# A smaller descriptor area for GpSimd's DMAs, and with it a lower start of every tile on the left side of SBUF

## The chip, the cores and the metric

The kernel runs on one core of a Trainium2 chip. The metric is the device time of one execution in microseconds (us). Each engine works through its own list of instructions in order: TensorE (PE) multiplies, VectorE (DVE), ScalarE (ACT) and GpSimd (POOL) do the elementwise work, and SyncE (SP) issues most of the DMAs. They meet at semaphores. SBUF is the memory from which the engines work; an address in it is given below as a byte offset within one partition.

## What is computed

One layer of a streaming encoder on 2048 rows of 1024 numbers, in float32. A mixer with two groups of heads (differential attention, and a gated linear recurrence called HGRN2) is followed by an output projection with a residual, and that by a convolutional gated feed-forward with a second residual. Cut to its frame:

```python
h = _rmsnorm(x, ln1_w[l])
proj = h @ w_in[l]
...
o_diff = _diff_attention(dq, dk, dv, lam, lam_init, diff_subln_w[l])
...
o_hgrn = _hgrn2(..., hg, lb, hgrn_norm_w[l])
x = x + jnp.concatenate([o_diff, o_hgrn], axis=-1) @ w_out[l]
x = x + _conv_ffn(_rmsnorm(x, ln2_w[l]), w_up[l], conv_w[l], conv_b[l], w_down[l])
```

In the attention a row sees all chunks of 64 rows up to its own, so the last block of rows has the most to do.

## The kernel before

The program has four stages, each with its own set of tile pools.

1. **The mixer** (lines 200 to 546). Four passes `s` over the heads; in each pass eight blocks `b` of 256 rows. `proj_a`, `proj_b` and `proj_c` are the input projections (L269 to L271), `attn` makes the scores `sc` of a block of 128 rows in segments of up to 1024 columns (L379, L380), takes their negated maximum `nm` on DVE (L387) and the exponential `p` on ACT (L398). There is one `sc` buffer (`SCB` is 1), so the scores of the next segment wait until the exponential has read this one. `attn_o` mixes the two softmaxes (L425, DVE), transposes the result (L431, PE), copies it (L433, ACT) and multiplies it with the values (L436, PE); the norm of the result goes over ACT (L440), POOL (L103, L105) and DVE (L443, L444), and L445 stores 128 columns of it in `o_d[i]`. `hgrn` and `hgrn_o` (L447 to L510) do the recurrence and store into the same `o_d[i]` by L510.
2. **The output projection** (lines 549 to 634). For each block `i` of 128 rows `load_o` loads `o_d[i]` into `ot` (L564) and the rows of x into `xt` (L566), transposes `ot` (L572) and splits it into a high and a low part `oT` (L577, L578). 48 matmuls (L621 to L623, two halves of 24) multiply it with `w_out`, L624 adds the residual on DVE, L625 stores the sum, and L628, L103, L105 and L630 make its norm `ht`. `tail` transposes `ht` (L590) and scales it into `hs` (L593). The eight row groups of `w_out` are split by `prep_wo` (L196 on ACT, L197 on DVE or POOL), seven of them late in the mixer, into tiles that held the projection weights, and the eighth (`wo7`, line 558) into a tile of its own.
3. **The up projection and the convolution** (lines 641 to 744), and 4. **the down projection** (lines 747 to 889). In stage 4 L838 adds partial results to `x2_d` in HBM by DMAs that POOL issues with `accum_op`; these 48 are the only DMAs of the program that POOL issues.

The order in which the instructions of each engine stand isn't that of the Python code: the build moves instructions of a later stage forward between those of an earlier one, as far as tiles and operands allow. A pool is laid at the left end of SBUF (from low addresses up) or at the right end (from high addresses down, `side="right"`). Pools of a later stage take addresses that pools of an earlier stage held; with `reuse_waits="tile"` (L84) a tile that takes over bytes waits for the last use of the tiles that had them.

```python
wk = pool(ms, "wk", 2, side="right")          # L206, mixer
sm = pool(ms, "sm", 4, side="right")          # L207, mixer: its small tiles
hp = pool(ms, "hp", 2, side="right")          # L210, mixer: hT
wp = pool(ms, "wp2", 1)                       # L551, output projection: wo7
wk = pool(ms, "wk2", 1)                       # L552: ot, xt, oT, ht
sm = pool(ms, "sm2", 4)                       # L553: ss2, r2_m, r2_r
```

At address 0 lies the area in which the descriptors of POOL's DMAs are written; the left pools begin behind it. `bacc.Bacc` takes its size per partition as `dynamic_dma_scratch_size`, 16384 where nothing is said.

## Time and profile before

| | us |
|---|---|
| three timed runs | 2781.37, 2786.12, 2788.0 (median 2786.12) |
| the profiled execution | 2784.47 |
| span of the profiled execution | 2782.5 |
| PE busy | 2651.1 (95%) |
| DVE, ACT, POOL busy | 1900.4 (68%), 1262.0 (45%), 1053.8 (38%) |

The page divides the span into 40 slices of 69.6 us and gives the busy tenths of each engine and the TensorE clock that was granted, in tenths of full speed. Matmul ends are modelled and overlap the next start, so for PE the distance between two starts tells what one costs.

### The profile page before, as it was taken

To read this page: it belongs to the slowest core of one execution; us is meant where nothing else is said; L and a number is where in the kernel's file an instruction comes from. 1 tells how busy PE (TensorE), PEld (TensorE's weight loads), DVE (VectorE), ACT (ScalarE), POOL (GpSimd) and SP (SyncE) were. 2 spreads that over 40 slices of the span, in tenths; PEclk is the share of its full clock that TensorE was granted. 3 is DMA by queue.
4 is the path that set the end of the run, shared out by engine and by line. 5 is a ranking of instruction groups with operands and counts; after the bars stand their busy time and mean duration, and the time that the engine had idled before them with its cause. 6 is when DMAs were issued, how large, how long until landed. Compare 5 with 4: busy or idle time off the path is not lost. (4 is left out here: it accounts for less than half of the span.)

```text
span 2782.5 us, 42697 instructions
## 1 busy us (share of the span) xinstructions
PE 2651.1 (95%) x14722; PEld 2303.3 (83%) x14722; DVE 1900.4 (68%) x4058; ACT 1262.0 (45%) x3095; POOL 1053.8 (38%) x1168
## 2 busy tenths in 40 slices
PE   7999999999999999969999999999999998899999
PEld 6888899989999999858877888887888886687887
DVE  5667856676568666752337666669677678977787
ACT  5556544564456445532334443435344344434332
POOL 3221222222222222310325344343443446887775
PEclk9999999999999999979999999999999999999999
DMA  5323422242223232114765222225222224775754
GB/s 190 121 97 111 132 85 88 80 133 84 84 84 112 85 114 83 51 37 152 237 204 159 82 78 91 79 81 176 90 91 72 88 89 120 166 165 132 174 173 171
DMA packets 273492, 322.92 MB, mean 116 GB/s; under 512 B 19470, under 2 KB 238974, under 8 KB 269182
## 3 DMA queue, kind: packets, MB, share of 16 engines
q1 hardware_dynamic: 266366, 295.04, 32.4%
q0 software_dynamic: 6912, 25.17, 5.3%
q8 instruction: 117, 1.92, 0.3%
q14 instruction: 97, 0.79, 0.1%
HBM read 198.50 MB, written 104.86 MB: 109 GB/s over the span
## 5 line engine op out<-in xcount | busy, mean ns | idle before, releaser
L706 PE MATMUL q<-xT,WS 128*128 128x512 f32 x704 | 274.1, 389 | 1.6 <-DVE xT L639 1.6
L707 PE MATMUL q<-xT,WS 128*128 128x512 f32 x704 | 274.2, 389 | 0.6 <-DVE WS L639 0.6
L705 PE MATMUL q<-xT,WS 128*128 128x512 f32 x704 | 274.0, 389 | 0.7 <-ACT WS L638 0.7
L819 PE MATMUL pd<-TW,SG 128*128 128x512 f32 x616 | 244.7, 398 | 19.6 <-DVE acc L825 6.7
L821 PE MATMUL pd<-TW,SG 128*128 128x512 f32 x616 | 243.0, 395 | 3.3 <-DVE SG L639 3.3
L820 PE MATMUL pd<-TW,SG 128*128 128x512 f32 x616 | 243.7, 396 | 0.9 <-DVE TW L639 0.7
L638 ACT CAST WS<-st 128x512 fp32r<-128x512 f32 x176 | 108.4, 618 | 240.9 <-PE q L707 229.7
L706 PE MATMUL q<-xB,WS 128*128 128x512 f32 x528 | 206.5, 391 | 2.6 <-DVE xB L639 2.5
L705 PE MATMUL q<-xB,WS 128*128 128x512 f32 x528 | 206.6, 391 | 2.3 <-ACT xB L638 2.3
L707 PE MATMUL q<-xB,WS 128*128 128x512 f32 x528 | 205.9, 390 | 0.0
L398 ACT ACTIVATE p<-sc,nm 128x1024 f32<-128x1024 f32 (+4 forms) x192 | 165.4, 862 | 76.8 <-DVE nm L387 75.7
L639 POOL TENSOR_TENSOR WS<-st,WS 128x512 fp32r<-128x512 f32 x44 | 87.5, 1989 | 278.9 <-ACT WS L638 278.9
L387 DVE TENSOR_REDUCE nm<-sc 128x1 f32<-128x1024 f32 (+4 forms) x192 | 173.9, 906 | 12.6 <-PE sc L380 10.7
L269 PE MATMUL pj<-WA,hT 128*128 128x384 f32 x512 | 176.6, 345 | 2.6 <-DVE hT L256 2.6
L270 PE MATMUL pj<-WA,hT 128*128 128x384 f32 x512 | 174.6, 341 | 0.0
L271 PE MATMUL pj<-WA,hT 128*128 128x384 f32 x512 | 174.5, 341 | 0.0
L436 PE MATMUL av<-vst,aT 128*128 128x128 f32 x1088 | 152.7, 282 | 8.2 <-ACT aT L433 7.8
L819 PEld LDWEIGHTS pd<-TW,SG 128*128 128x128 f32 x616 | 117.7, 191 | 49.8 <-DVE acc L825 8.1
L706 PEld LDWEIGHTS q<-xT,WS 128*128 128x128 f32 x704 | 132.1, 188 | 29.7 <-DVE xT L639 2.5
L707 PEld LDWEIGHTS q<-xT,WS 128*128 128x128 f32 x704 | 132.1, 188 | 28.8 <-DVE WS L639 1.5
L705 PEld LDWEIGHTS q<-xT,WS 128*128 128x128 f32 x704 | 132.1, 188 | 28.6 <-ACT WS L638 1.2
L638 ACT CAST WS<-rawu 128x512 fp32r<-128x512 f32 x132 | 81.9, 622 | 161.1 <-PE q L707 159.9
(441 smaller groups left out, 7896.3 us busy)
## 6 DMA issues: line engine op xcount, KB each, us to landing
hT<-hTd SPq DMA_DIRECT2D x24, 2048.0 KB, 7.9
rawu<-in_w_up_dram SPq DMA_DIRECT2D x176, 256.0 KB, 3.1
x2d<-acc POOLq DMA_DIRECT2D x48, 512.0 KB, 6.5
gd<-c SPq DMA_DIRECT2D x176, 128.0 KB, 1.8
G<-gd SPq DMA_DIRECT2D x24, 768.0 KB, 4.3
hTd<-hT SPq DMA_DIRECT2D x8, 2048.0 KB, 6.2
qT<-qh SPq DMA_DIRECT2D x256, 64.0 KB, 2.0
rawd<-in_w_down_dram SPq DMA_DIRECT2D x22, 512.0 KB, 4.4
```

Source lines behind the costliest of these rows:

```text
L269: PE.matmul(dst, lhsT=lh, rhs=rh, start=dt == 0, stop=False)
L270: PE.matmul(dst, lhsT=lh, rhs=rl, start=False, stop=False)
L271: PE.matmul(dst, lhsT=ll, rhs=rh, start=False, stop=dt == ND - 1)
L387: DVE.tensor_reduce(out=nm, in_=sc[:, 0:w], axis=AX.X, op=ALU.max, negate=True)
L398: ACT.activation(out=p[:, 0:w], in_=sc[:, 0:w], func=AF.Exp, bias=nm, accum_out=l)
L638: ACT.copy(dst[:, 0], src)
L705: PE.matmul(dst, lhsT=w[:, 0, cs], rhs=b_[:, 0, dt], start=dt == 0, stop=False)
L706: PE.matmul(dst, lhsT=w[:, 0, cs], rhs=b_[:, 1, dt], start=False, stop=False)
L707: PE.matmul(dst, lhsT=w[:, 1, cs], rhs=b_[:, 0, dt], start=False, stop=dt == 3)
L819: PE.matmul(pd, lhsT=Sx[n][:, 0, k], rhs=w[:, 0], start=k == 0, stop=False)
L820: PE.matmul(pd, lhsT=Sx[n][:, 0, k], rhs=w[:, 1], start=False, stop=False)
L821: PE.matmul(pd, lhsT=Sx[n][:, 1, k], rhs=w[:, 0], start=False, stop=k == len(qs) - 1)
```

## The change

The descriptor area takes 8192 bytes per partition. Nothing else in the text of the kernel is touched.

```diff
-    nc = bacc.Bacc("TRN2", target_bir_lowering=False, num_devices=1)
+    nc = bacc.Bacc("TRN2", target_bir_lowering=False, num_devices=1, dynamic_dma_scratch_size=8192)
```

All left pools of all stages start 8192 bytes lower; the right pools stay. As the build lays the tiles out, in bytes of a partition:

| pool | side, stage | before | with the change |
|---|---|---|---|
| `hp` (`hT`) | right, mixer | 94208 to 126976 | the same |
| `sm` (small tiles) | right, mixer | 133440 to 136164 | the same |
| `wp2` (`wo7`) | left, output projection | 93184 to 101376 | 84992 to 93184 |
| `wk2`: `ot`, `xt`, `oT` | left, output projection | 101376 to 130048 | 93184 to 121856 |
| `wk2`: `ht` | left, output projection | 130048 to 134144 | 121856 to 125952 |
| `sm2` | left, output projection | 134336 to 134628 | 126144 to 126436 |

So `ht` and `sm2` no longer share bytes with the mixer's `sm`, and `wo7` no longer with `hT`. `ot`, `xt` and `oT` share bytes with `hT` before and after. All offsets move by a multiple of 512 bytes, the unit to which `Rows` (L41 to L59) rounds its tiles.

The order of the instructions changes in one place of the program, the end of the mixer's last pass and the start of the output projection. On all engines it is the same before and behind it. Three pieces:

PE, in the scores of the last rows of the mixer (`sc`, L379 and L380; `lt`, L465, is the recurrence; `pjo` is the output projection, here of block 0):

```order
 L379 MATMUL sc<-kst,qT 128x384
 L380 MATMUL sc<-kst,qT 128x384
+L621 MATMUL pjo<-woWA,oT 128x512
+L622 MATMUL pjo<-woWA,oT 128x512
+L623 MATMUL pjo<-woWA,oT 128x512
+L621 MATMUL pjo<-woWA,oT 128x512
+L465 MATMUL lt<-qP,kp 128x128
+L622 MATMUL pjo<-woWA,oT 128x512
+L623 MATMUL pjo<-woWA,oT 128x512
```

All 48 matmuls of block 0 now stand among the last score groups: 15 between this group and the next, then 13, 10, 9, and the last one behind the scores. Before, none of them stood ahead of the mixer's last matmul.

PE, the end of the mixer (`av`, L436, is its last product; `tpo` are the transposes of `load_o`, `tph` those of `tail`):

```order
 L431 MATMUL tpa<-ident,p 128x128 x8
+L590 MATMUL tph<-ident,ht 128x128 x2
 L436 MATMUL av<-vst,aT 128x128 x8
-L572 MATMUL tpo<-ident,ot 128x128 x8
+L590 MATMUL tph<-ident,ht 128x128 x6
 L621 MATMUL pjo<-woWA,oT 128x512
 L622 MATMUL pjo<-woWA,oT 128x512
```

Behind the mixer's last product there now come six transposes of block 0's `tail` and then the matmuls of block 1, whose own transposes (L572) stand ahead of it.

SP, the stores of the mixer's last rows (`od` numbered by block of 128 rows, `rawu` a load for stage 3) and the loads of the output projection (`ot` from `od_97` and `xt` for block 0, `od_98` for block 1):

```order
+L668 DMA rawu<-in_w_up_dram 128x4x128 x2
+L445 DMA od_109<-oo 128x128
+L564 DMA ot<-od_97 128x1024
+L566 DMA xt<-in_x_dram 128x1024 x2
 L668 DMA rawu<-in_w_up_dram 128x4x128
-L445 DMA od_109<-oo 128x128
-L668 DMA rawu<-in_w_up_dram 128x4x128 x2
 L510 DMA od_109<-o_16488 128x128
+L564 DMA ot<-od_98 128x1024
 L445 DMA od_110<-oo 128x128
 L510 DMA od_110<-o_16511 128x128
+L510 DMA od_111<-o_16834 128x128
```

Before, the loads L564 and L566 all came behind the store of `od_112`, the mixer's last; now three of them stand right behind the store of `od_109`, and that of `ot` for block 1 two rows on. On ACT and DVE the cast and the difference of `wo7` (L196, L197) move ahead by some ten instructions, and the splits, sums and the norm of block 0 (L577, L578, L624, L628, L630) now stand among the last instructions of `attn`.

## Rows read from the trace of the kernel before

**Rows 1.** From the page's 40 slices: PE, and the granted clock of TensorE.
```profile
PE   7999999999999999969999999999999998899999
...
PEclk9999999999999999979999999999999999999999
```

**Rows 2.** Windows: start and end, length, busy us (count) per engine, PEclk, DMA share, GB/s.
```profile
1200.00:1210.00 10.00, 5.94 (x16) 4.40 (x16) 6.46 (x23) 2.77 (x7) 0.74 (x2) 0.59 0.04 13
1210.00:1220.00 10.00, 6.80 (x19) 5.19 (x20) 8.29 (x27) 2.48 (x5) 0.00 (x0) 0.50 0.01 2
1220.00:1230.00 10.00, 8.90 (x59) 7.94 (x58) 4.84 (x16) 5.60 (x15) 0.74 (x2) 0.89 0.00 0
1230.00:1240.00 10.00, 5.79 (x27) 4.92 (x28) 5.69 (x13) 3.18 (x9) 3.39 (x4) 0.62 0.07 20
1240.00:1250.00 10.00, 5.35 (x34) 4.92 (x33) 0.51 (x2) 1.53 (x4) 0.74 (x2) 0.84 0.11 29
```

**Rows 3.** Waits of PE from 1188.5 to 1254.5: total us, times, longest.
```profile
PE tpo L572 <- DMA ot<-od: 6.3, 1, 6.3
...
PE sc L379 <- ACT p L398: 3.5, 2, 3.3
```

**Rows 4.** Timeline of PE: start, us, instruction, idle before it and its releaser.
```profile
1243.53 2.05 PE L436 MATMUL av<-vst,aT 128*128 128x128 f32 x16 [0.24 <-ACT aT L433]
1251.90 1.97 PE L572 MATMUL tpo<-ident,ot 128*128 128x128 f32 x8 [6.32 <-DMA ot<-od]
1254.42 0.79 PE L621 MATMUL pjo<-woWA,oT 128*128 128x512 f32 x1 [0.55 <-DVE oT L578]
...
1262.51 0.39 PE L621 MATMUL pjo<-woWA,oT 128*128 128x512 f32 x1
...
1267.95 0.60 PE L572 MATMUL tpo<-ident,ot 128*128 128x128 f32 x4
...
1269.31 0.47 PE L621 MATMUL pjo<-woWA,oT 128*128 128x512 f32 x1
...
1275.09 1.03 PE L590 MATMUL tph<-ident,ht 128*128 128x128 f32 x8
1275.88 0.48 PE L622 MATMUL pjo<-woWA,oT 128*128 128x512 f32 x1
```

**Rows 5.** Timeline of SP: DMA issues.
```profile
1191.28 0.92 SPq L668 DMA_DIRECT2D rawu<-in_w_up_dram  x2
...
1247.65 0.32 SPq L445 DMA_DIRECT2D od<-oo  x1
1248.02 0.42 SPq L564 DMA_DIRECT2D ot<-od  x1
```

**Rows 6.** Timeline of PE: the last score matmul of a segment and the next segment's first.
```profile
1213.72 0.63 PE L380 MATMUL sc<-kst,qT 128*128 128x512 f32 x1
...
1217.15 0.80 PE L379 MATMUL sc<-kst,qT 128*128 128x512 f32 x1
```

**Rows 7.** Timelines of DVE and PE: single instructions whose lengths are used.
```profile
1196.29 1.22 DVE L197 TENSOR_TENSOR wo<-raw,wo 128x1024 fp32r<-128x1024 f32 x1
...
1233.88 2.47 DVE L425 SCALAR_TENSOR_TENSOR p<-p,cc 128x1024 f32<-128x1024 f32 x2
...
1253.67 0.69 DVE L578 TENSOR_TENSOR oT<-tpo,oT 128x512 fp32r<-128x512 f32 x1 [6.05 <-ACT oT L577]
...
1236.49 1.94 PE L431 MATMUL tpa<-ident,p 128*128 128x128 f32 x8 [1.71 <-DVE p L425]
1238.26 3.78 PE L436 MATMUL av<-vst,aT 128*128 128x128 f32 x16
```

**Rows 8.** The page's queue of POOL's DMAs, and the issues of L838.
```profile
q0 software_dynamic: 6912, 25.17, 5.3%
...
L838 POOL DMA_DIRECT2D x2d<-acc x48: 861/1128/1197, 2352.9 to 2676.3; - x48
...
DMA to landing us min/median/max: 5.2/6.5/11.2
```

## The prediction, on record before the changed kernel ran

> **What bounds the kernel now.** I read the page first. PE is busy nine tenths or more in nearly every slice, at full clock nearly everywhere; the one dent in both lies in the 18th slice, 1183 to 1252 us [rows 1]. Where PE is dense, a change pays only if it takes work or idle time off PE. So the next view is the windows of PE there: from 1200 to 1250 it is busy 5.4 to 8.9 us of each ten, and the granted clock is 0.50 to 0.89 of full [rows 2]. This is the place that the change touches: the mixer's last rows, where its other work has run out.
>
> The waits say what holds PE there: one hole of 6.3 us for the load of `ot`, and waits for a chain through DVE and ACT, the longest 3.3 for an exponential [rows 3]. The timelines put them in order. The mixer's last product ends at 1243.53 + 2.05 = 1245.58; PE then stands until 1251.90 and transposes block 0 [rows 4]. The load was issued at 1248.02, on SP right behind the store of the mixer's last rows at 1247.65 [rows 5]: the output projection begins only when the mixer is over. Its first 24 matmuls take from 1254.42 to 1262.51, 8.09 us, the next 24 until 1267.95, 5.44 or 0.227 each [rows 4]. The second is the full clock of 2.4 GHz; the first was paid partly at 1.2 GHz, the level of the window 1210 to 1220 [rows 2].
>
> **The change, term by term**, from the profiled execution (2784.47 us; the median of the timed runs lies 1.65 higher).
>
> *What leaves the path: 24.5 us.* Block 1's matmuls begin at 1269.31. In the new order they follow the mixer's last product with only six transposes (L590) between, and the eight L590 of block 0, which stood inside block 1's matmuls for 1275.88 - 1275.09 = 0.79 [rows 4], have moved ahead too. So 1269.31 + 0.79 - 1245.58 = 24.52 us lie between the two points: the wait for the mixer's last norm and store, the load, the transposes and block 0's 48 matmuls.
>
> *What comes back there: 0.8 us,* the eight L590; 1.6 at half clock.
>
> *The clock at block 1's start: 0.5 us.* Block 0 lost 8.09 - 5.44 = 2.65 to the low clock. Block 1 follows the mixer's products without a hole, and of these the last 16 took 2.05 [rows 4] where the 16 before them took 3.78 [rows 7]: PE was back at full some 2 us ahead of its end. I take 0.5 and keep 0 and 2.6 as ends.
>
> *The mixer's tail itself: 1 us earlier.* Here 48 matmuls and 16 transposes (L572) are put among the scores. From the last score matmul of one segment to the first of the next (DVE's maximum and ACT's exponential lie between) PE has 1217.15 - 1213.72 - 0.63 = 2.8 us free [rows 6]. The groups of 15, 13, 10 and 9 moved matmuls need 3.4, 3.0, 2.3 and 2.0 us at 0.227; with 0.3 for `lt` the first two overflow, by 0.9 and 0.5. Against that, filled holes should give the full clock: four score matmuls then take 4 x 0.227 = 0.9 us less per segment, and four segments ran at half (0.59 and 0.50 from 1200 to 1220 [rows 2]): 3.6 back. On DVE two splits (L578) and two sums (L624), 0.69 each [rows 7], come among the maxima; DVE is idle a third of 1200 to 1230 [rows 2], and I count one of them on the chain, 0.7. In front, the difference of `wo7` (1.22 [rows 7]) now stands ahead of the mixing of an earlier block; it no longer stands where it stood, so 0.5 net. 3.6 - 1.4 - 0.7 - 0.5 = 1.0; the bounds are 3 earlier and 2 later.
>
> *SP.* The load of `ot` moves past the stores of three blocks of rows. Ahead of it stands the pair of `rawu`, which waited for DVE until 1191.28 [rows 5] and now waits some 1 us more for the later difference. Issued near 1193.3 and landing about 3.9 us later (1251.90 - 1248.02 [rows 4, 5]), it lets the first transpose go at about 1197. That one stands in PE's list between a score group's two halves and what precedes them; PE stands some 2 us, but DVE's next maximum waited for the norm of earlier rows as well, so I leave it within the bounds above. The stores that now follow the load wait for later data in any case. Block 1's load waits for block 0's transposes near 1200 and has 30 us of cover. POOL takes two small norm steps ahead of the last recurrence's, whose store nothing of the path waits for; the cast of `wo7` on ACT moves ahead by some 10 us, and its data were issued well before.
>
> *Behind it.* PE is busy nine tenths and more at full clock in nearly all later slices [rows 1], and the order of all engines is unchanged to the end, so a shift at block 1 goes through. The area itself: 48 transfers of 6912 / 48 = 144 packets [rows 8]; I cost its halving at nothing (below).
>
> Sum: 24.5 - 0.8 - 0.5 + 1.0 = 24.2 us less; 2784.47 - 24.2 = 2760.3, rounded **2760 us**. The bounds give 24.5 - 1.6 - 2.6 - 2 = 18.3 to 24.5 - 0.8 + 3 = 26.7: 2757.8 to 2766.2.
>
> **Rivals.**
>
> *Full clock throughout.* The 16 transposes and 32 products behind the scores run at full too. Half of them were at half clock: 1.94 for eight transposes and 3.78 for 16 products against 2.05 [rows 4, 7], so 0.97 + 1.73 = 2.7 less. 24.2 + 0.5 + 2.7 = 27.4: 2757. For it: PE was granted 0.89 as soon as it was busy 8.9 of 10 [rows 2]. Against it: DVE's two mixings (2.47 us from 1233.88 [rows 7]) leave PE empty ahead of these products in either order. The Trainium skill, "TensorE: Matmul & The Clock Gate", section "What's actually happening", says that the throttled state is the default and activity releases it; by that rule alone the filled tail would be at full and this rival the forecast. The trace agrees with the release but shows the fall too, at every such hole.
>
> *The tail falls to half and stays there: no change.* PE stands some 2 us for the first load near 1195, much as it stood 3.3 [rows 3] before the low clock of 1200 to 1220 [rows 2]. Then 48 matmuls cost 48 x 0.454 = 21.8 us and 16 transposes at 1.94 / 8 another 3.9. PE's idle time from 1200 to 1245.6 is 45.6 - 32.8 = 12.8 [rows 2]. If all of it is filled, the tail ends 25.7 - 12.8 = 12.9 later: 24.5 - 12.9 - 1.9 (L590 at half) = 9.7 gained, 2775. If none is, 24.5 - 25.7 - 1.9 = -3.1: 2788. The middle, 3.3, is no change: 2781. Against it: block 0's dense matmuls had the clock back after 2.65 / 0.227 = 12 of them [rows 4].
>
> *The area fills: slower.* If half the area holds only one transfer's descriptors, POOL must wait until the first transfer of each pair has landed before it can write the second's. The place is L838, the price 6.5 us to landing less the 1.13 of its own issue, 24 times: 129 us of POOL. As no row shows what slack takes up, I count half of it as passing to PE: 64, so 2849. It decides from the point where a transfer needs over half of the 8192 bytes. Against it: 144 packets over 16 engines are 9 per engine, and transfers 6.7 us apart (323 us for 48) that land in 6.5, at most 11.2, are one or two in flight [rows 8]. How many bytes that is no row shows; the Trainium skill, "DMA: Bandwidth & Descriptors", sections "Terms" and "The descriptor swizzle", gives 16 bytes a descriptor and, for 1 MiB, nine per side and engine, by which two such transfers are an estimated 576 bytes per engine and nothing would wait.
>
> That the change doesn't do what it says is excluded by the order, whose pieces show the moved rows.
>
> **How the numbers follow.** Forecast 0.66, full clock 0.22, half clock 0.09, filled area 0.03. I take 0.3% (8.4 us) as what a measurement can tell from no change. Faster: forecast, full clock and 0.03 of the half-clock case (its good end): 0.91. Same: the rest of that case, 0.06. Slower: 0.03. The range takes the forecast's bounds and the full-clock case, with the timed runs' spread of some 3 us on either side: 2754 to 2769; outside lie the half-clock case and the filled area, 0.12.
>
> **What would show it.** Right: L572 and L621 of block 0 among the scores between 1195 and 1230; the windows 1200 to 1230 over 9 us busy and near full clock; no hole of 6 us behind the mixer; block 1's first matmul near 1246 instead of 1269; equal distances between later marks; L838 landing in 6.5 us. Wrong: the mixer's last product later than 1248 (half clock, or PE held by a load), a second wait for `ot`, or POOL idle at L838.

## The result, and the profile after

| | before | after |
|---|---|---|
| timed runs, median (range), us | 2783.74 (2781.33 to 2788.0, 4 runs) | 2755.85 (2753.56 to 2759.65, 4 runs) |
| profiled execution, us | 2784.47 | 2754.72 |
| its span, us | 2782.5 | 2753.0 |

The ratio of the times is 0.99, with a 95% interval of 0.9881 to 0.9918: 27.9 us less by the medians, where 24 were forecast (2760 us, range 2754 to 2769).

The page's slices of the changed kernel, to be held against [rows 1]: the dent of PE in the 18th slice is an 8 where it was a 6, and the clock has no 7 left.

```profile
PE   7998999999999999989999999999999998899999
...
PEclk9999999999999999999999999999999999999999
```

The windows of the same stretch as [rows 2]; columns as there (busy time of PE, of its weight loads, of DVE, ACT and POOL, then the granted clock, DMA share and GB/s):

```profile
1200.00:1210.00 10.00, 8.07 (x49) 6.53 (x48) 7.16 (x21) 4.53 (x13) 1.94 (x5) 1.00 0.24 72
1210.00:1220.00 10.00, 10.00 (x50) 8.38 (x49) 8.97 (x36) 2.48 (x5) 0.00 (x0) 1.00 0.01 2
1220.00:1230.00 10.00, 9.99 (x72) 8.89 (x71) 7.32 (x18) 5.84 (x15) 0.74 (x2) 1.00 0.03 8
1230.00:1240.00 10.00, 6.42 (x38) 5.47 (x37) 6.84 (x15) 5.04 (x14) 3.67 (x6) 0.85 0.52 168
1240.00:1250.00 10.00, 9.98 (x62) 8.77 (x61) 0.51 (x2) 3.69 (x12) 0.74 (x2) 0.98 0.20 62
```

From 1200 to 1230 PE is at full clock, and from 1210 full, where it had 5.9 to 8.9 us of each ten at 0.50 to 0.89. What is left is a wait in the first window and a longer hole in that from 1230. The waits of PE from 1185 to 1262 name both (total us, times, longest):

```profile
PE tpa L431 <- DVE p L425: 3.1, 2, 2.1
PE sc L379 <- ACT p L398: 1.7, 1, 1.7
PE sp L499 <- ACT op L507: 0.9, 1, 0.9
...
```

The wait of 6.3 us for `ot` of [rows 3] isn't there. In the timeline of PE (start, us, instruction, idle before it):

```profile
1185.03 0.47 PE L379 MATMUL sc<-kst,qT 128*128 128x512 f32 x1
...
1198.25 0.27 PE L572 MATMUL tpo<-ident,ot 128*128 128x128 f32 x1
...
1204.65 0.50 PE L379 MATMUL sc<-kst,qT 128*128 128x512 f32 x1 [1.71 <-ACT p L398]
...
1205.36 0.42 PE L379 MATMUL sc<-kst,qT 128*128 128x384 f32 x1
...
1205.79 0.39 PE L621 MATMUL pjo<-woWA,oT 128*128 128x512 f32 x1
...
1218.13 0.46 PE L379 MATMUL sc<-kst,qT 128*128 128x512 f32 x1
...
1222.12 0.48 PE L379 MATMUL sc<-kst,qT 128*128 128x512 f32 x1
...
1235.77 1.07 PE L431 MATMUL tpa<-ident,p 128*128 128x128 f32 x8 [2.09 <-DVE p L425]
1237.08 3.61 PE L436 MATMUL av<-vst,aT 128*128 128x128 f32 x16 [0.24 <-ACT aT L433]
...
1241.81 2.05 PE L436 MATMUL av<-vst,aT 128*128 128x128 f32 x16
1243.70 0.82 PE L590 MATMUL tph<-ident,ht 128*128 128x128 f32 x6
1244.27 0.47 PE L621 MATMUL pjo<-woWA,oT 128*128 128x512 f32 x1
...
1249.84 0.39 PE L621 MATMUL pjo<-woWA,oT 128*128 128x512 f32 x1
```

Block 0's matmuls (the first L621 at 1205.79) run among the scores, the mixer's last product ends at 1241.81 + 2.05 = 1243.86, and block 1 starts at 1244.27, at full clock from its first matmul: 24 of them take until 1249.84, 5.57 us.

**Where the time came from.** The two executions don't reach the changed stretch at the same moment, though nothing ahead of it was changed. So I measure from the last scores ahead of it that both orders share: 1182.01 before, 1185.03 after. Four more rows of PE before the change are needed:

```profile
1182.01 0.47 PE L379 MATMUL sc<-kst,qT 128*128 128x512 f32 x1
...
1203.57 0.67 PE L379 MATMUL sc<-kst,qT 128*128 128x384 f32 x1
...
1219.02 1.06 PE L431 MATMUL tpa<-ident,p 128*128 128x128 f32 x4
...
1223.37 0.48 PE L379 MATMUL sc<-kst,qT 128*128 128x512 f32 x1
```

One pair of executions can mislead, so three more stand beside it in the table: experiment 1 below has the order of before, in experiment 8 the change itself ran again, and experiment 6 has the order of the change. Their marks, last products and block 1's first matmuls, in this order of runs (of the change run again also the transposes of the last rows):

```profile
1180.63 0.47 PE L379 MATMUL sc<-kst,qT 128*128 128x512 f32 x1
...
1240.53 2.05 PE L436 MATMUL av<-vst,aT 128*128 128x128 f32 x16 [0.24 <-ACT aT L433]
...
1265.67 0.48 PE L621 MATMUL pjo<-woWA,oT 128*128 128x512 f32 x1
```

```profile
1179.27 0.48 PE L379 MATMUL sc<-kst,qT 128*128 128x512 f32 x1
...
1230.08 1.94 PE L431 MATMUL tpa<-ident,p 128*128 128x128 f32 x8 [2.10 <-DVE p L425]
...
1237.04 2.05 PE L436 MATMUL av<-vst,aT 128*128 128x128 f32 x16
...
1239.50 0.47 PE L621 MATMUL pjo<-woWA,oT 128*128 128x512 f32 x1
```

```profile
1182.87 0.48 PE L379 MATMUL sc<-kst,qT 128*128 128x512 f32 x1
...
1241.33 2.05 PE L436 MATMUL av<-vst,aT 128*128 128x128 f32 x16
...
1243.79 0.47 PE L621 MATMUL pjo<-woWA,oT 128*128 128x512 f32 x1
```

| us after the common mark | before | experiment 1 | after | the change again | experiment 6 |
|---|---|---|---|---|---|
| the score group behind the longest wait for the exponential (1202.27; after: 1204.65) | 20.26 | 20.27 | 19.62 | 19.64 | 19.63 |
| its first matmul of 384 columns | 21.56 | 21.45 | 20.33 | 20.35 | 20.93 |
| the score segment three on (1217.15, [rows 6]; 1218.13) | 35.14 | 35.02 | 33.10 | 33.17 | 34.22 |
| the next segment (1223.37; 1222.12) | 41.36 | 40.27 | 37.09 | 37.16 | 38.20 |
| transposes of the last rows (1236.49, [rows 7]; 1235.77) | 54.48 | 53.85 | 50.74 | 50.81 | 51.85 |
| end of the mixer's last product | 63.57 | 61.95 | 58.83 | 59.82 | 60.51 |
| block 1's start (in the order of before with 0.79 for the L590 inside it) | 88.09 | 85.83 | 59.24 | 60.23 | 60.92 |

In the first pair block 1 starts 28.85 us earlier: 4.7 are a shorter mixer tail, and 24.1 are work and holes that no longer stand between the mixer's last product and block 1 (24.52 before, 0.41 after). Over all six pairs of the table (two executions of the old order, three of the new) the second part is 23.5 to 24.1; the shorter tail is 1.4 to 4.7, 3.0 in the mean. So the second part is firm, and of the first only the sign and the rough size are.

### The profile page after: what moved, and what is told of

It reads as the page before. It is cut to its first block, busy times and chain, and to the rows that moved or that the text cites. A ratio compares the mean times of both kernels' runs of the same rounds, so it can differ in the third digit from the quotient of the medians.

```text
span 2753.0 us, 42693 instructions
## 1 busy us (share of the span) xinstructions
PE 2639.6 (96%) x14722; PEld 2297.4 (83%) x14722; DVE 1896.5 (69%) x4058; ACT 1262.7 (46%) x3095; POOL 1055.5 (38%) x1168
## 5 line engine op out<-in xcount | busy, mean ns | idle before, releaser
L705 PE MATMUL q<-xT,WS 128*128 128x512 f32 x704 | 274.3, 390 | 0.7 <-ACT WS L638 0.7
L705 PE MATMUL q<-xB,WS 128*128 128x512 f32 x528 | 206.7, 392 | 2.9 <-ACT xB L638 2.9
L436 PE MATMUL av<-vst,aT 128*128 128x128 f32 x1088 | 153.9, 284 | 6.9 <-ACT aT L433 6.5
L705 PEld LDWEIGHTS q<-xT,WS 128*128 128x128 f32 x704 | 132.2, 188 | 28.5 <-ACT WS L638 1.2
```

Source lines behind the costliest of these rows:

```text
L705: PE.matmul(dst, lhsT=w[:, 0, cs], rhs=b_[:, 0, dt], start=dt == 0, stop=False)
```

## The experiments

Each ratio is to runs of the kernel before on the same chip.

**1. The area alone.** A pad tile that lies at the left end of SBUF in all stages grows by what the area lost, so every tile lies where it lay before.

```diff
-TOP, FEW, SMALL, SMALL2 = 480, 128, 320, 192
+TOP, FEW, SMALL, SMALL2 = 480, 128 + 8192, 320, 192
```

> The 8192-byte area, with 8192 bytes of padding at the left end, so that every tile lies where it lay before; the order of all engines is that of before. Theory (the gain comes from the tiles that no longer share bytes with the mixer's small tiles, and so from block 0's work moving into the mixer's tail): no change, 2784 us within 0.3%, the hole of 6 us behind the mixer is there and block 1's matmuls start some 87 us behind the same mark. Rival (the smaller area itself does something, as less descriptor memory or other addresses): up to the whole 28 us of the change are seen here; or, if the area fills, some us slower with L838 landing later than 6.5 us.

Measured: 2782.95 us (12 runs), ratio 1.0002, 0.999 to 1.0015. The order is that of before, and so is the hole:

```profile
1248.70 1.97 PE L572 MATMUL tpo<-ident,ot 128*128 128x128 f32 x8 [6.12 <-DMA ot<-od]
```

The size of the area by itself does nothing. The gain lies in the tiles' places.

**2. Only `wo7` free.** A pad of 8192 bytes ahead of `ot` puts `ot`, `xt`, `oT`, `ht` and `sm2` back to their places of before; `wo7` stays clear of `hT`.

```diff
-        wk = pool(ms, "wk2", 1)
+        wk = pool(ms, "wk2", 1); wk.tile([P, 2048], F32, name="padw")
```

> The change with 8192 bytes of padding inside the second pool of the output projection: the tile wo7 is clear of hT as with the change, but ot, xt, oT, ht and the small tiles lie where they lay before. Theory (the small tiles decide): no gain, 2784 within 0.3%. Rival (wo7 and its earlier cast and difference decide): most of the 28 us.

Measured: 2782.56 us (12 runs), ratio 0.9991, 0.998 to 1.0001, and PE waits 6.3 us for `ot`. The early split of `wo7` is worth nothing that can be told from the time.

**3. `wo7` bound, the small tiles free.** With an area of 12288 bytes all left pools move down by 4096: `ht` and `sm2` are clear of the mixer's small tiles, `wo7` (to 97280) still shares bytes with `hT` (from 94208).

```diff
-dynamic_dma_scratch_size=8192)
+dynamic_dma_scratch_size=12288)
```

> An area of 12288 bytes: all left tiles lie 4096 bytes lower than before, so ht and the small tiles of the output projection are clear of the mixer's small tiles, but wo7 still shares bytes with hT and its cast and difference stand late. Theory: nearly all of the gain, 2754 to 2762. Rival (wo7's early place is needed): less than half of it, 2770 or more.

Measured: 2754.78 us (5 runs), ratio 0.9899, 0.9884 to 0.9915. The whole gain, without `wo7`.

**4. Down by 1024 bytes.** The same edit with 15360. Now `ht` ends at 133120, ahead of the small tiles (from 133440), while `sm2` still shares bytes with them.

> An area of 15360 bytes: the left pools move 1024 bytes down instead of 8192. ht then ends at 133120, clear of the mixer's small tiles (from 133440); sm2 still shares bytes with them, and wo7 with hT. Theory (what counts is that ht, which holds the norm of a block of rows, is clear of the small tiles): 2753 to 2761 us, no hole of 6 us behind the mixer's last product. Rival (sm2's tiles must be clear as well): 2779 to 2788, with the hole for the load of ot.

Measured: 2756.6 us (4 runs), ratio 0.9899, 0.9884 to 0.9915. So it was `ht`: its 4096 bytes reached 134144 - 133440 = 704 bytes into the mixer's small tiles, and with that the norm of block 0, which is written to `ht`, was bound to the mixer's end. `sm2` and `wo7` may stay bound. Why the loads and the matmuls of block 0, which don't touch `ht`, stayed behind with the norm is a matter of how the build moves instructions; no run shows its rule.

**5. The loads and transposes early, the matmuls not.** `EARLY` at 0 keeps the 48 matmuls of block 0 behind the mixer; the loads of `ot` and 24 transposes (L572, of blocks 0 to 2) are still in the tail.

```diff
-EARLY, TP, LO, HSB, HVB, XTB = 1, 1, 2, 5, 3, 2
+EARLY, TP, LO, HSB, HVB, XTB = 0, 1, 2, 5, 3, 2
```

> The change with EARLY = 0: block 0's matmuls take their PSUM from the pool that follows the scores' PSUM, so they can't go into the mixer's tail; its loads and transposes still can. Theory (48 matmuls move into PE's holes, and by filling them keep the clock at full): the hole behind the mixer is gone, but the 48 matmuls, 11 us at 0.227, come back there, and the tail runs at half clock again and ends some 4 us later than with the change; 12 to 17 us slower than with the change, so 2768 to 2773. Rival (the gain is the load's hole and the clock at block 0's start alone, the matmuls could as well stay): within 3 us of the change, 2756 to 2759, and the mixer's last product as early as there.

Measured: 2763.13 us (6 runs), ratio 0.9929, 0.9914 to 0.9944. Neither number that I had written holds it: 20.7 of the 28 us come without the matmuls in the tail. The windows show what I had missed:

```profile
1200.00:1210.00 10.00, 6.47 (x31) 4.91 (x29) 7.73 (x24) 5.04 (x13) 0.74 (x2) 0.83 0.37 118
1210.00:1220.00 10.00, 6.67 (x40) 5.09 (x40) 9.55 (x30) 4.20 (x8) 0.00 (x0) 1.00 0.18 55
```

PE is busy about as long as before there (6.47 and 6.67 us against 5.94 and 6.80), but at 0.83 and 1.00 of full clock, where the kernel before was granted 0.59 and 0.50 [rows 2]. And what follows the mixer starts at once:

```profile
1241.10 2.05 PE L436 MATMUL av<-vst,aT 128*128 128x128 f32 x16 [0.24 <-ACT aT L433]
1242.91 0.47 PE L621 MATMUL pjo<-woWA,oT 128*128 128x512 f32 x1
```

From this kernel's mark (1182.79) to the end of the last product are 60.36 us: within the 58.83 to 60.51 of the change's order, and 1.6 to 3.2 less than in the order of before. So the shorter tail comes without the matmuls too, as far as its spread lets one tell. Hiding the 48 matmuls (10.9 us at 0.227) gave the remaining 7.3 by the medians; against experiment 3, on the same chip, it is 8.4.

**6. A smaller area still.** The change with 2048 bytes; the order on all engines is that of the change.

> The change with a descriptor area of 2048 bytes instead of 8192; the order of every engine is that of the change. Theory (the area's size itself is free; L838 is never held for room): 2752 to 2759 us, the 48 issues of L838 landing in 6.2 to 6.6 us median, POOL without a wait at them. Rival (a small area holds back the second transfer of a pair): L838 landing later or POOL idle ahead of it, and the time over 2765, up to 2849.

Measured: 2756.91 us (4 runs), ratio 0.9898, 0.9878 to 0.9918. The view of L838, first of the change, then of this kernel (duration in ns, least, median and longest, first and last start):

```profile
L838 POOL DMA_DIRECT2D x2d<-acc x48: 868/1126/1217, 2323.3 to 2646.8; - x48
...
DMA to landing us min/median/max: 5.2/6.3/11.5
```

```profile
L838 POOL DMA_DIRECT2D x2d<-acc x48: 871/1133/1227, 2323.3 to 2647.3; - x48
...
DMA to landing us min/median/max: 5.2/6.3/11.1
```

Issue and landing are those of before ([rows 8]: 1128 ns, 6.5 us). Even an eighth of the area holds nothing back here.

**7. Block 1 between the last products.** `EARLY` at 2, an attempt to fill the hole that is left.

> The change with EARLY set to 2: matmuls of block 1 may stand between the mixer's last products as well; only PE's order differs, by some thirty rows, among them one or two L621 of block 1 ahead of the last av. Theory (behind the scores PE loses only the wait for the last mixing on DVE, some 2 us, and the low clock after it, which one matmul does not fill): within 2 us of the change, 2752 to 2758. Rival (matmuls of block 1 keep the clock up over the last products): 1.5 us and more below the change, 2748 to 2753.

Measured: 2758.99 us (4 runs), ratio 0.991, 0.9894 to 0.9927: not below the change's order, which had 2756.91 on the same chip, and the wait of 2.1 us for L425 stays. One matmul doesn't fill it. The time is 1 us above the range of the theory (2752 to 2758) and far from the rival's.

**8. Block 1's load first.** `LO` at 0 puts the load and transposes of each next block ahead of a block's matmuls.

```diff
-EARLY, TP, LO, HSB, HVB, XTB = 1, 1, 2, 5, 3, 2
+EARLY, TP, LO, HSB, HVB, XTB = 1, 1, 0, 5, 3, 2
```

> The change with LO set to 0: the load and the transposes of block 1 stand ahead of block 0's matmuls among the scores; the scores' order around them changes too. Theory (PE's work is the same and the tail is already dense from 1200 to 1230, so another order gives nothing): 2752 to 2760. Rival (block 1's transposes fill holes and come off the place behind the mixer): 2 us and more below the change, 2748 to 2752; or, if the transposes hold PE for the later load, a hole for ot among the scores and 2760 to 2768.

Measured: 2747.92 us (4 runs), ratio 0.9869, 0.9854 to 0.9884; on the same chip the change's order had 2756.91. That is below the 2752 to 2760 of the theory that another order gives nothing. It was run again beside the change itself:

> The change itself, unedited, beside the next three. Both theories: 2752 to 2759 us; it gives the distance to the version with LO at 0 on one chip.

> The change with LO at 0, as before, now beside the change. From the last score segment that both orders share to the end, the two traces differed by some 1 us only (1567.0 against 1567.4), the rest lay ahead of it, where the orders are the same. Theory (most of the 8 us between the medians is the spread of runs): 0 to 3 us below the change. Rival (the order with LO at 0 is really better): 5 us and more below the change, with their medians' ranges apart.

Measured: the change 2751.81 (4 runs, 2749.25 to 2759.2), ratio 0.9902, 0.9884 to 0.9921; `LO` at 0 2748.64 (4 runs, 2743.4 to 2755.0), ratio 0.9888, 0.9868 to 0.9908. The distance is 3.2 us here and was 9.0 there; it lies between the two expectations and decides for neither. The traces speak for some 3: from block 1's start to the first L705 on `xT` in the up projection the change's order takes 195.7, 197.3 and 196.9 us in three executions (the last that of experiment 6), `LO` at 0 takes 193.8 and 192.9. A small gain is likely, its size stays open. With `EARLY` at 2 as well:

> LO at 0 and EARLY at 2 together on the change's layout; against LO at 0 alone only PE's order differs, by some thirty rows of blocks 0 to 2. Theory (PE is dense there and only changes places): within 3 us of LO at 0 alone. Rival (PE's transposes of block 1 no longer ahead of their operands, or ahead of them): 3 us or more to either side.

Measured: 2749.84 us (5 runs, 2743.95 to 2757.34), ratio 0.9894, 0.9876 to 0.9913: no further gain.

**9. Block 1's load first, without the change.** `LO` at 0 and the area of 16384 bytes.

> LO at 0 with the descriptor area of 16384 bytes, so without the change: the load of ot for block 0 and the 48 matmuls stay behind the mixer, only block 1's transposes move ahead of block 0's matmuls. Theory (LO pays only where the tail has room): the 6 us hole for ot stays, 2780 to 2788 us. Rival (LO at 0 saves by itself, as it takes block 1's transposes from between dense matmuls): 2774 to 2780.

Measured: 2785.39 us (11 runs), ratio 1.0013, 1.0003 to 1.0024. Behind the mixer PE now waits for two loads before its first matmul:

```profile
1258.42 1.97 PE L572 MATMUL tpo<-ident,ot 128*128 128x128 f32 x8 [6.17 <-DMA ot<-od]
1263.76 0.45 PE L572 MATMUL tpo<-ident,ot 128*128 128x128 f32 x1 [3.37 <-DMA ot<-od]
```

The same setting pays nothing, or a little less than nothing, where the loads can't move into the mixer.

## Why the prediction was right, and which term was mis-sized

**The place and the main term held.** "What leaves the path: 24.5 us" less the 0.8 of the eight L590 is 23.7; measured are 23.5 to 24.1. Experiments 1, 3 and 4 tie it to the moved tiles.

**The mixer's tail was mis-sized:** 1.0 us forecast with 3 as the upper bound, 4.7 measured in the first pair and 1.4 to 4.7 over all pairs. It shows in the time: by the medians 27.9 us were saved, more than the 26.7 of the forecast's own bounds, so 2755.85 lies below their 2757.8, and inside the stated range only by what that adds for the full-clock case and the spread. The table says where the term went wrong.

- *In front,* the moved difference of `wo7` was charged 0.5. The score group behind it starts 0.6 earlier instead, to within 0.02 in every execution of either order; the exponential is waited for 1.71 us there instead of 3.3 [rows 3]. It is `wo7`'s place that does this: with only `wo7` free (experiment 2, mark at 1180.36) the same group starts at 19.02, and with `wo7` bound and `ht` free (experiments 3 and 4) at 20.74 and 20.49.

```profile
1199.38 0.50 PE L379 MATMUL sc<-kst,qT 128*128 128x512 f32 x1 [1.52 <-ACT p L398]
```

- *The clock of that group* came back in two of three executions: its first matmuls take 0.71 us up to that of 384 columns where they took 1.30 and 1.18, but 1.30 in experiment 6.
- *Over the three segments that follow* the sum came out: 0.8 in the first pair, 0.3 to 0.8 over all, where a clock gain of 0.9 each, the overflow of 1.4 and DVE's 0.7 give 0.6. The single terms of that sum aren't shown.
- *Behind them* the order moved, and this I had not looked at. Before, eight transposes, `lt` and 16 products stood between one segment's scores and the next, in part at half clock (1219.02 to 1223.37, 4.35 us); in the new order the scores go first. The way from the one segment to the next takes 4.0 us in all three executions of the new order, and 6.2 and 5.3 in those of the old: 1.3 to 2.2 gained. I had read the order for added matmuls and not for score groups that changed places.
- *The last rows* are the part that is luck. In the first pair the last 8.1 us of the tail are 1.0 shorter than before, with the transposes at full clock (the first eight 1.07 instead of 1.94 us). In the second execution of the same kernel these eight take 1.94 again and the last stretch 9.0, and in experiment 1, in the order of before, it takes 8.1.

**The clock at block 1's start** was charged 0.5 us; its first 24 matmuls took 5.57 against 5.44 [rows 4], so 0.1.

**SP.** I had read the pair of `rawu` as waiting for DVE until 1191.28 [rows 5] and had the load issued near 1193.3, landing with PE standing 2 us. In the changed kernel the second of the pair does wait for the difference of `wo7`, but only until 1190.62, ahead of the store. First the view of SP's waits, then its timeline with the second of the pair by itself:

```profile
SPq L668 <- DVE wo L197: 3.2, 1, 3.2
```

```profile
1190.62 0.37 SPq L668 DMA_DIRECT2D rawu<-in_w_up_dram  x1
1191.90 0.34 SPq L445 DMA_DIRECT2D od<-oo  x1
1192.29 0.43 SPq L564 DMA_DIRECT2D ot<-od  x1
```

The store of `od_109` goes 6.9 us behind the mark, and 6.8 before the change (1188.79), so the wait costs nothing. The load right behind it lies 7.3 us behind the mark; 1193.3 would have been 11.3. The first L572 at 1198.25 waits for nothing. I had left the stall out of the sum as a bound, so this cost no number, but the rival that began with that stall had no ground.

**Behind it** the profiles don't keep equal distances, as I had said they would. From block 1's start to the first L705 on `xT` took 1469.7 - 1270.1 = 199.6 us before and 195.7 after, from there to the end 1312.8 and 1313.0. The 3.9 us stem from one late `ht` in the execution before:

```profile
1394.83 1.97 PE L590 MATMUL tph<-ident,ht 128*128 128x128 f32 x8 [4.06 <-DVE ht L630]
1397.03 0.63 PE L622 MATMUL pjo<-woWA,oT 128*128 128x512 f32 x1
```

Its transposes start 1.7 us later behind block 1's start than after the change, where this wait is 2.48 us; from them to the next eight are 15.1 us instead of 12.8, with these eight at half clock. In the profiled executions of experiments 1 and 2, which have this stretch in the order of before, the wait is 2.47 and 2.30 us and the whole distance 195.8 and 195.6, so it is spread between executions, as are the 3.0 us of the other sign ahead of the mark. 28.85 + 3.9 - 3.0 - 0.2 = 29.5 is the difference of the two spans.

**The rivals.** *Full clock throughout* gave 2757, nearest of all to 2755.85, but its ground did not come true. Of the last rows' work that it counted, the first eight transposes ran at full in the execution shown (1.07), the 16 products did not (3.61 against 3.78 [rows 7]); in the second execution of the same kernel neither did (1.94 and 3.78). That its number is near is luck. PE was granted 0.85 in that window, behind the 2.09 us in which it stood for L425. The Trainium skill, "TensorE: Matmul & The Clock Gate", section "What's actually happening", has throttling as the default and activity as its release. The trace agrees in the filled windows, at 1.00, and at the hole of 2.09 us; behind the wait of 1.71 us the clock stayed at 1.00. *Half clock in the tail* fell: 1.00 from 1200 to 1230. *The area fills* fell with experiment 6: not even 2048 bytes are too few.

**What stays open.** The 48 matmuls alone, without the loads and transposes, can't be moved, so their share is known only on top of these (7.3 us of 27.9). How much shorter the mixer's tail is on average, five executions don't settle.

## What to carry to other kernels

Where an engine's order follows from which tiles share bytes, look in the address table for the smallest overlap between two stages: here 704 bytes of one tile held the start of a stage behind the end of the one before, and 1024 bytes were enough to free it. Measure two profiles from a mark that both orders share, as near ahead of the change as there is one, else spread elsewhere passes for a part of the effect; and set more than one pair side by side, for behind the mark too the tail came out 1.4 to 4.7 us shorter, by the pair. And read the difference of two orders for what changed places, not only for what was added: that was worth 1.3 to 2.2 us here.

## What the runs showed of the hardware

- The granted clock can't be read off PE's busy time: 0.50 at 6.80 us of ten [rows 2], 1.00 at 6.67 in experiment 5. At half clock the same work is busy for longer, and in these two windows PE ran 19 and 40 matmuls (of several sizes). Before, PE had stood 3.3 us for an exponential ahead of the low clock [rows 3]; in experiment 5 the longest such wait was 1.72 us, the clock fell behind it too (0.63 us instead of 0.39 for a score matmul), and was back some four us later, during eight transposes that now stood between the scores (1.35 us, where eight take 1.03 at full and 1.94 at half). In the changed kernel it did not fall behind the same wait of 1.71 us, and in experiment 6 it did.
- The same hole is not always followed by the low clock. Behind the 2.09 and 2.10 us for L425 the eight transposes of the last rows take 1.07 us in one execution of the changed kernel and 1.94 in another. In the same two PE waits for `ht` at the same place, 2.48 and 2.60 us, and the eight transposes behind it take 1.09 and 1.97:

```profile
1367.28 1.09 PE L590 MATMUL tph<-ident,ht 128*128 128x128 f32 x8 [2.48 <-DVE ht L630]
```

```profile
1362.64 1.97 PE L590 MATMUL tph<-ident,ht 128*128 128x128 f32 x8 [2.60 <-DVE ht L630]
```

- The common mark, ahead of which all orders are the same, is reached between 1177.7 (experiment 8's second run) and 1191.5 us (experiment 9) in the profiled executions. The timed runs of one kernel are about as wide (2743.4 to 2755.0 for `LO` at 0), so a difference of 3 us, as between the last two versions, asks for more runs than these.
